# Split inputs computed ahead and kept in DRAM, the seven-product down projection in block one too, and the sample's modulation sums moved to the projections of blocks two and three

## The chip, the cores and the metric

The kernel runs on one core of a Trainium2 chip. TensorE (PE) multiplies, VectorE (DVE), ScalarE (ACT) and GpSimd (POOL) work elementwise, and SyncE (SP) only issues DMAs; POOL issues DMAs too. Every engine takes its instructions strictly in order, so an instruction that waits holds back all that stands behind it on that engine. The metric is the device time of one execution in microseconds (us), the median of several.

## The reference

One layer of a streaming encoder. A prompt of 2048 tokens and a sample of 64 tokens, each with its own conditioning vector `c`, go through the same weights:

```
mod = silu(c) @ w_ada + b_ada                 # sh1, sc1, g1, sh2, sc2, g2, 1024 each
hn  = rms(x) * (1 + sc1) + sh1
q, f, iv, og, xr, gr = split(hn @ w_in)       # 1024 -> 3072
o_hg = hgrn2(q, f, iv) * gain * silu(og)      # 4 heads of 128, chunks of 64, a state per head
o_rg = rglru(conv(xr)) * gelu(gr)             # width-4 conv, gated linear recurrence
x = x + g1 * (concat(o_hg, o_rg) @ w_out)
x = x + g2 * (relu(hn2 @ w_up)**2 @ w_down)   # hn2 = rms(x) * (1 + sc2) + sh2; 1024 -> 4096 -> 1024
y = rms(x) * final_gain
```

All of it is float32 at a tight tolerance.

## The kernel before, in words

**Split products.** A float32 matrix product is made of three passes over two rounded parts, hi and lo, of each operand (hi·hi, hi·lo, lo·hi). `Split` holds such a pair. Weights are split by ACT (hi, line 244) and DVE or POOL (lo, line 245) out of a raw tile; the split parts of `w_in` and `w_out` are stored to DRAM in block 0 (`kept_in`, `kept_out`) and read back by POOL's queue in the later blocks (`load_kept`, 1 MB each, a ring of six weight tiles `wt`).

**Blocks.** The prompt runs in four blocks b = 0 to 3 of 512 tokens; the title counts them from one, all else by b. The sample rides along in the last. A block has these stages: the input XT (normalised, modulated, split); the projections (`hg_proj` for q and f, `hg_vo` for iv and og, `rg_in`, `rg_out`, lines 651 and 768) with the HGRN chain of each head between them (on PE lines 821 to 905, on DVE a level-by-level chain over seven doubling levels, lines 846 to 858); the output projection and second norm (`phase_O`); the MLP in eight groups g of 512 hidden columns, each with an up projection U(g) (`phase_U`, 96 matmuls of 128x512) and, one group later, its down projection D(g). I call what is left of a block's D work after U(7), up to the next block's first projection, its tail.

**Down projection.** In block 0 `phase_D0` does it plainly: 96 matmuls per group, each of eight PSUM results added to `acc` by DVE (line 1069). In blocks 1 to 3 `phase_W` does it with seven products of half-size blocks in place of eight: 84 matmuls per group (line 1098), with sums of the operand made by `sums_of`, differences of the weights by `down_units` (line 1037), and 14 additions into `acc` and `accM` on DVE (line 1087). `combine` (line 1116) adds these at the end. The last block's last group is plain.

**The next block's input.** `phase_A1` takes the square sums of the next block's x during U(5). `phase_A`, which stands in the tail, multiplies the reciprocal norms out with four matmuls (line 530, `ps_rs`), loads x transposed (`x_t`), and writes hi and lo of XT: per 128 columns one DVE scalar_tensor_tensor (line 540), one ACT activation (541) and another DVE scalar_tensor_tensor (542), 8 of each. They can only begin when U(7) has read the old XT.

**Modulation.** Sums over `w_ada` are made on DVE: a raw tile of 512 KB is multiplied by silu(c) and added up (`ada_first` line 288, `ada_part` line 333, 128x1024), and at the end PE sums over partitions with narrow matmuls against a vector of ones (lines 303 and 337). Part G2 of the prompt's and all six of the sample's (`ada_s`) run in block 0's MLP, eleven steps behind each of the groups 1 to 6, with raw tiles from a ring of two (`rowp`).

**Order.** Each stage has a rank (`sec(b, rank)`); a scheduler sorts every engine's stream by it and by what is ready, so its result is read from the order of instructions, not from the source. SP issues the loads of raw weights, of x and of `w_ada` in order; POOL issues the kept weights.

Of the kernel before, what the change touches and what calls it, by code (L numbers as in the profile page):

```python
# [129 lines left out]
def hymba_step(ctx: ExitStack, tc: tile.TileContext, i: dict, o: dict):  # L130
# [376 lines left out]
    def phase_A1(B, after=None):  # L507

        ss = smp.tile([P, 8], F32, tag="ss", name="ss_a")
        for t in range(4):  # L510
            x = x_load(xp[B.toks[t][4]:B.toks[t][4] + P], P, after)
            S.activation(x, x, AF.Square, accum_out=ss[:, t:t + 1])
        V.tensor_scalar(ss[:, 0:4], ss[:, 0:4], 1.0 / D, EPS, op0=ALU.mult, op1=ALU.add)
        B.rs = rsqrt(ss, P, 4)

    def phase_A(B, after=None):


# [8 lines left out]
        hd = hdp.tile([P, 2560], F32, tag="hd", name="hd_a")  # L527
        ps = pax.tile([P, 512], F32, tag="ax", name="ps_rs")
        for t in range(4):
            T.matmul(ps[:, t * P:(t + 1) * P], lhsT=B.rs[:, t:t + 1].to_broadcast([P, P]), rhs=ident, start=True, stop=True)  # L530
        rb = hd[:, 0:BLK]
        xts = [x_load(i["x_t"][B.b, k2], P, after, hd[:, k2 * D - 1536:k2 * D - 512] if k2 > 1 else None) for k2 in range(4)]
        S.copy(rb, ps)
        for k2 in range(4):
            x = xts[k2].rearrange("p (k t) -> p k t", k=2)
            for kk in range(2):
                k = 2 * k2 + kk
                sc, sh = modc[:, SC1, 0, k:k + 1], modc[:, SH1, 0, k:k + 1]
                hi, lo = (y[:, k, :BLK] for y in B.XT.p)
                V.scalar_tensor_tensor(x[:, kk], x[:, kk], sc, rb, op0=ALU.mult, op1=ALU.mult)  # L540
                S.activation(hi, x[:, kk], AF.Identity, bias=sh)
                V.scalar_tensor_tensor(lo, x[:, kk], sh, hi.bitcast(F32), op0=ALU.add, op1=ALU.subtract)
# [797 lines left out]
```

## Time and profile before

| | us |
|---|---|
| median of 3 runs | 2664.72 (2662.12 to 2667.94) |
| the profiled execution | 2663.96 |
| its span, first to last instruction | 2662.1 |
| mean granted TensorE clock | 0.965 of 2.4 GHz |
| TensorE busy | 2468.7 (93%) |
| VectorE busy | 1812.4 (68%) |

The span is what the trace covers; 1.9 us of the execution lie outside it. TensorE's share says that nearly all time is matmuls or waits of matmuls: a stage gets shorter if its matmuls get fewer or if something that TensorE waits for comes sooner. Stages are read from TensorE's timeline, which gives the first matmul of each.

### The profile page before, as it was taken

To read this page: it belongs to the slowest core of one execution; us is meant where nothing else is said; L and a number is where in the kernel's file an instruction comes from. 1 tells how busy PE (TensorE), PEld (TensorE's weight loads), DVE (VectorE), ACT (ScalarE), POOL (GpSimd) and SP (SyncE) were. 2 spreads that over 40 slices of the span, in tenths; PEclk is the share of its full clock that TensorE was granted. 3 is DMA by queue.
4 is the path that set the end of the run, shared out by engine and by line. 5 is a ranking of instruction groups with operands and counts; after the bars stand their busy time and mean duration, and the time that the engine had idled before them with its cause. 6 is when DMAs were issued, how large, how long until landed. Compare 5 with 4: busy or idle time off the path is not lost.

```text
span 2662.1 us, 33130 instructions
## 1 busy us (share of the span) xinstructions
PE 2468.7 (93%) x12792; PEld 2071.5 (78%) x12792; DVE 1812.4 (68%) x3248; ACT 1026.8 (39%) x1640; POOL 191.5 (7%) x245
## 2 busy tenths in 40 slices
PE   5888899999899999999899999999799998999997
PEld 4667688788787778888677778888678877998976
DVE  7587666766544756878954756878954566568787
ACT  4334252322212336455312336455312524644432
POOL 2311100000011100000001100000011110000000
PEclk8999899999999999999999999999899999999998
DMA  8564735766355332234445332234353533222213
GB/s 337 213 218 155 292 119 199 240 208 208 132 184 205 112 135 84 99 111 166 151 173 211 106 135 83 100 111 146 135 201 127 104 127 131 80 87 88 87 65 107
DMA packets 96414, 397.35 MB, mean 149 GB/s; under 512 B 14432, under 2 KB 16384, under 8 KB 79360
## 3 DMA queue, kind: packets, MB, share of 16 engines
q1 hardware_dynamic: 79696, 274.63, 30.1%
q0 software_dynamic: 16560, 120.59, 12.5%
q8 instruction: 101, 1.65, 0.3%
q14 instruction: 57, 0.47, 0.0%
HBM read 343.77 MB, written 51.41 MB: 148 GB/s over the span
## 4 chain that ended last, share of the span: by engine, by line
PE 66%; DVE 15%; issue 9%; DMA 5%; ACT 4%; POOL 1%; SPq 0%; DVEq 0%; POOLq 0%; ACTq 0%
PE ps_u L1012 24%; PE ps_d L1098 14%; PE ps_in L651 7%; PE ps_d L1064 5%; PE ps_vo L768 4%; PE ps_y L938 3%; DVE wt L245 2%; PE ps_lv L842 2%; DMA raw<-in_w_ada_dram 2%; PE ps_in L636 1%; DMA wt<-kept_in 1%; PE ps_rg L712 1%; PE ps_s L1108 1%; DVE ada_acc L333 1%; DVE ada_acc L288 1%
## 5 line engine op out<-in xcount | busy, mean ns | idle before, releaser
L1012 PE MATMUL ps_u<-XT,wt 128*128 128x512 f32 (+2 forms) x4128 | 749.9, 342 | 18.1 <-ACT XT L399 5.4
L1012 PEld LDWEIGHTS ps_u<-XT,wt 128*128 128x128 f32 x4128 | 658.2, 190 | 101.6 <-ACT XT L399 6.8
L245 DVE TENSOR_TENSOR wt<-raw,wt 128x1024 fp32r<-128x1024 f32 x338 | 414.0, 1237 | 251.6 <-ACT wt L244 220.2
L244 ACT CAST wt<-raw 128x1024 fp32r<-128x1024 f32 x357 | 371.6, 1048 | 316.9 <-PE ps_d L1064 87.1
L651 PE MATMUL ps_in<-XT,wt 128*128 128x512 f32 (+1 forms) x1776 | 376.5, 360 | 13.2 <-POOL wt L245 4.0
L651 PEld LDWEIGHTS ps_in<-XT,wt 128*128 128x128 f32 x1776 | 288.5, 190 | 58.8 <-issue 5.5
L1098 PE MATMUL ps_d<-wt,gS 128*128 128x512 f32 x1104 | 261.6, 395 | 27.2 <-DVE accM L1087 22.8
L1098 PEld LDWEIGHTS ps_d<-wt,gS 128*128 128x128 f32 x1104 | 210.7, 191 | 73.3 <-DVE accM L1087 23.6
L938 PE MATMUL ps_y<-wt,mix 128*128 128x512 f32 x800 | 207.1, 415 | 21.8 <-ACT wt L244 8.4
L1015 ACT ACTIVATE hd_u<-ps_u 128x512 f32<-128x512 f32 (+2 forms) x172 | 85.2, 497 | 343.8 <-PE ps_u L1012 340.0
L768 PE MATMUL ps_vo<-wt,XT 128*128 128x512 f32 x800 | 207.1, 409 | 2.5 <-POOL wt L245 1.6
L938 PEld LDWEIGHTS ps_y<-wt,mix 128*128 128x128 f32 x800 | 156.2, 199 | 61.5 <-ACT wt L244 8.7
L1098 PE MATMUL ps_d<-wt,gA 128*128 128x512 f32 x828 | 196.2, 390 | 0.0
L1064 PE MATMUL ps_d<-wt,gt 128*128 128x512 f32 x768 | 181.0, 396 | 8.3 <-DVE acc L1069 8.3
L1098 PEld LDWEIGHTS ps_d<-wt,gA 128*128 128x128 f32 x828 | 154.9, 188 | 32.0 <-DVE acc L1087 0.2
L1064 PEld LDWEIGHTS ps_d<-wt,gt 128*128 128x128 f32 x768 | 146.9, 192 | 39.9 <-DVE acc L1069 8.9
L768 PEld LDWEIGHTS ps_vo<-wt,XT 128*128 128x128 f32 x800 | 150.2, 195 | 32.3 <-POOL wt L245 1.9
L1037 DVE TENSOR_TENSOR raw<-raw 128x1024 f32<-128x1024 f32 x92 | 113.5, 1233 | 2.2
L1087 DVE TENSOR_TENSOR acc<-acc,ps_d 128x512 f32<-128x512 f32 x160 | 106.2, 681 | 1.7 <-PE ps_d L1098 0.6
L842 PEld LDWEIGHTS ps_lv<-hd_h 128*128 128x128 f32 x640 | 85.6, 204 | 27.5 <-issue 17.7
L1087 DVE TENSOR_TENSOR accM<-accM,ps_d 128x512 f32<-128x512 f32 x120 | 79.9, 681 | 36.5 <-PE ps_d L1098 35.8
L842 PE MATMUL ps_lv<-hd_h 128*128 128x64 f32 x640 | 88.9, 285 | 13.8 <-DVE hd_h L847 11.8
(308 smaller groups left out, 2646.6 us busy)
## 6 DMA issues: line engine op xcount, KB each, us to landing
wt<-kept_in POOLq DMA_DIRECT2D x72, 1024.0 KB, 7.4
raw<-in_w_up_dram SPq DMA_DIRECT2D x128, 512.0 KB, 3.3
raw<-in_w_down_dram SPq DMA_DIRECT2D x128, 512.0 KB, 3.3
raw<-in_w_ada_dram SPq DMA_DIRECT2D x80, 512.0 KB, 4.2
wt<-kept_out POOLq DMA_DIRECT2D x24, 1024.0 KB, 5.1
kept_in<-wt POOLq DMA_DIRECT2D x19, 1024.0 KB, 9.0
raw<-in_w_in_dram SPq DMA_DIRECT2D x24, 512.0 KB, 7.2
x_a<-in_x_prompt_dram SPq DMA_DIRECT2D x16, 512.0 KB, 4.8
```

The lines of the kernel that those rows point to most:

```text
L244: S.copy(wt[:, 0], raw)
L245: eng.tensor_tensor(wt[:, 1], raw, wt[:, 0].bitcast(F32), op=ALU.subtract)
L651: T.matmul(ps[:, :pn], lhsT=w[:, a, k], rhs=B.XT.p[x][:, k, p0:p0 + pn], start=(k == 0 and q == 0), stop=(k == KD - 1 and q == 2))
L768: T.matmul(ps[:rows(B.toks[ti])], lhsT=l, rhs=ws[k // 2][:, a, k % 2], start=(q == 0), stop=(q == len(ops) - 1))
L842: T.matmul(ps[:C, c * C // 2:(c + 1) * C // 2].rearrange("p (b h) -> p b h", h=hs), lhsT=KS[:, c * C:c * C + C], rhs=qv[:, c * bc:(c + 1) ...
L938: T.matmul(ps[:rows(B.toks[ti])], lhsT=l, rhs=ws[k - k % 2][:, a, k % 2], start=(q == 0), stop=(q == len(ops) - 1))
L1012: T.matmul(ps[:, :pn], lhsT=w[:, a, k], rhs=B.XT.p[x][:, k, p0:p0 + pn], start=(k == 0 and q == 0), stop=(k == KD - 1 and q == 2))
L1015: S.activation(r, ps[:, :pn], AF.Relu)
L1037: V.tensor_tensor(d, x, y, op=ALU.subtract)
L1064: T.matmul(ps, lhsT=l, rhs=ws[half][c // 2][:, a, c % 2], start=(q == 0), stop=(q == len(ops) - 1))
L1087: return V.tensor_tensor(dst, dst, ps, op=ALU.add)
L1098: T.matmul(ps, lhsT=op[x][y][:, c, t * P:(t + 1) * P], rhs=w[:, a, c], start=(k == 0), stop=(k == len(ops) - 1))
```

## The change

Three things move.

1. `phase_D0` goes; block 0 uses `phase_W` and `combine` like the others.
2. `keep_A` computes the hi and lo parts of the next block's input ahead, one 128-column step at a time (load, DVE, ACT, DVE, store), and stores them to DRAM (`kept_x`, 4 MB a block). For block 1 it runs in block 0's MLP, four steps a group (G2 after it), with tiles of another ring of two (`xap`) and the stores on POOL's queue; for blocks 2 and 3 in the projections of blocks 1 and 2, with tiles of the ring of three raw weights and the stores on SP's queue. `phase_A` is then eight loads of 512 KB on POOL's queue (and the sample's own norm in the last block).
3. The sample's six modulation parts leave block 0's MLP. `ada_sample(1)` and `ada_sample(2)` make half of them each in the projections of blocks 1 and 2: 24 raw tiles of 512 KB through the same ring of three, 48 DVE operations of 128x512, six sums on PE. G2 of the prompt stays in block 0's MLP.

```diff
+    def ada_sample(b):
+        accs = adp.tile([P, 2, 512], F32, tag="ada", name="ada_acc")
+        def fin(h, acc):
+            ps = pmd.tile([P, 512], F32, tag="md", name="ps_ada")
+            if h < 4:
+                for m in range(2):
+                    for j in range(2):
+                        T.matmul(ps[:, 2 * m + j:2 * m + j + 1], lhsT=acc[:, (2 * j + m) * P:(2 * j + m + 1) * P],
+                                 rhs=ones, start=True, stop=True)
...
+        hs = range(6 * b - 6, 6 * b)
+        for h in hs:
+            acc = accs[:, h % 2]
+            for k0 in range(0, KD, 2):
+                raw = rawp.tile([P, 1024], F32, tag="raw", name="raw")
...
+                for k in range(2):
+                    ck = silc[:, 1, k0 + k:k0 + k + 1]
+                    if k0 + k == 0:
+                        V.tensor_scalar(av, rv[:, k], ck, None, op0=ALU.mult)
+                    else:
+                        V.scalar_tensor_tensor(av, rv[:, k], ck, av, op0=ALU.mult, op1=ALU.add)
+                if k0 == 4 and h > hs[0]:
+                    with sec(b, 13):
+                        fin(h - 1, accs[:, 1 - h % 2])
+        with sec(b, 13):
+            fin(hs[-1], acc)
...
-    def phase_A1(B, after=None):
+    def keep_A(B, pool_, tag, rbp, eng, at):
         ss = smp.tile([P, 8], F32, tag="ss", name="ss_a")
...
+        for k in range(KD):
+            t = pool_.tile([P, 2, BLK], F32R, tag=tag, name="x_k")
+            x, hi = t[:, 0].bitcast(F32), t[:, 1]
+            Q.dma_start(x, i["x_t"][B.b, k // 2][:, k % 2 * BLK:k % 2 * BLK + BLK])
+            sc, sh = modc[:, SC1, 0, k:k + 1], modc[:, SH1, 0, k:k + 1]
+            V.scalar_tensor_tensor(x, x, sc, rb, op0=ALU.mult, op1=ALU.mult)
+            S.activation(hi, x, AF.Identity, bias=sh)
+            V.scalar_tensor_tensor(t[:, 0], x, sh, hi.bitcast(F32), op0=ALU.add, op1=ALU.subtract)
+            eng.dma_start(B.kept[k // 2][:, :, k % 2], t.bitcast(F32))
+            yield
...
     def phase_A(B, after=None):
         B.XT = Split(xtp, "xt", KD, "XT1")
+        for k2 in range(4):
+            for q in range(2):
+                G.dma_start(B.XT.p[q][:, 2 * k2:2 * k2 + 2, :BLK], B.kept[k2][:, 1 - q])
...
-        plain = B.b == 0 or B.last and g == DFF // 512 - 1
+        plain = B.last and g == DFF // 512 - 1
...
-    def phase_D0(B, g, gt):
...
-    ada_s = [ada_part(G2, 0), ada_first(1)] + [ada_part(p, 1) for p in range(2, 6)]
+    ada_0 = [keep_A(blocks[1], xap, "xa", (adp, "ada"), G, ExitStack)] if NB > 1 else []
+    ada_0.append(ada_part(G2, 0, own=True))
...
+        if 0 < b < NB - 1:
+            keep_b = [keep_A(blocks[b + 1], rawp, "raw", (adp, "ada"), Q, lambda: sec(b, 13))]
+            run(keep_b, 2)
...
+        if 0 < b < NB - 1:
+            with sec(b, 30):
+                run(keep_b, 99)
+                ada_sample(b)
...
-                        run(ada_s, 11)
+                        run(ada_0, 4)
...
-                if b:
-                    combine(B)
+                combine(B)
```

Where it moves instructions, three places show it. VectorE, in U(7) of block 1, where its tail begins, before (`hd_a` and `x_a` hold x of the next block, XT_9161 is its input; lines 971 to 975 and 966 are the sums of U(7)):

```order
L1037 TENSOR_TENSOR raw<-raw 128x1024 x2
L245 TENSOR_TENSOR wt<-raw,wt 128x1024 x2
L540 SCALAR_TENSOR_TENSOR x_a<-x_a,modc,hd_a 128x512 x3
L542 SCALAR_TENSOR_TENSOR XT_9161<-x_a,modc,XT_9161 128x512
L966 TENSOR_TENSOR gA_9139<-hd_u,gA_9139 128x512
L542 SCALAR_TENSOR_TENSOR XT_9161<-x_a,modc,XT_9161 128x512 x2
L540 SCALAR_TENSOR_TENSOR x_a<-x_a,modc,hd_a 128x512
L966 TENSOR_TENSOR gA_9142<-hd_u,gA_9142 128x512
L540 SCALAR_TENSOR_TENSOR hd_a<-hd_a,modc 128x512
L971 TENSOR_TENSOR hd_u<-hd_u 128x2x256
```

and now, at the same place (lines 1098, 1027, 1032 and 1127 are the old 1037, 966, 971 and 1087):

```order
L1098 TENSOR_TENSOR raw<-raw 128x1024 x2
L245 TENSOR_TENSOR wt<-raw,wt 128x1024
L1127 TENSOR_TENSOR accM<-accM,ps_d 128x512
L245 TENSOR_TENSOR wt<-raw,wt 128x1024
L1127 TENSOR_TENSOR accM<-accM,ps_d 128x512
L1027 TENSOR_TENSOR gA_9308<-hd_u,gA_9308 128x512
L245 TENSOR_TENSOR wt<-raw,wt 128x1024
L1127 TENSOR_TENSOR acc<-acc,ps_d 128x512
L1027 TENSOR_TENSOR gA_9311<-hd_u,gA_9311 128x512
L1127 TENSOR_TENSOR acc<-acc,ps_d 128x512
L1032 TENSOR_TENSOR hd_u<-hd_u 128x2x256
```

The sixteen scalar_tensor_tensor are gone, and the tail's additions (line 1127), the first of which came behind all sixteen, now begin among the sums of U(7).

VectorE, in the projections of block 1, where head 1's chain passes two of its levels, before (lines 846, 847 and 857 are the chain, line 708 the convolution):

```order
L846 TENSOR_TENSOR hd_h<-hd_h 128x32x8
L847 TENSOR_TENSOR hd_h<-hd_h 128x32x8
L857 COPY_PREDICATED hd_h<-masks,ps_lv 128x32x8
L846 TENSOR_TENSOR hd_h<-hd_h 128x16x16
L847 TENSOR_TENSOR hd_h<-hd_h 128x16x16
```

and now (907, 908, 918 and 769 are the old 846, 847, 857 and 708; line 365 is a step of a sum of the sample's modulation):

```order
L907 TENSOR_TENSOR hd_h<-hd_h 128x32x8
L908 TENSOR_TENSOR hd_h<-hd_h 128x32x8
L918 COPY_PREDICATED hd_h<-masks,ps_lv 128x32x8
L769 SCALAR_TENSOR_TENSOR rgtmp<-rgtmp,cols 128x512
L365 SCALAR_TENSOR_TENSOR ada_acc<-raw,silc,ada_acc 128x512
L907 TENSOR_TENSOR hd_h<-hd_h 128x16x16
```

Between two levels of the chain there is now an operation that waits for a raw tile.

TensorE at the same place, before (line 821 opens head 1's chain, 842 is a level of it):

```order
L651 MATMUL ps_in<-XT_4809,wt 128x512 x57
L821 MATMUL ps_dg<-hd_h 128x128 x4
L651 MATMUL ps_in<-XT_4809,wt 128x512 x5
L842 MATMUL ps_lv<-hd_h 128x64 x4
L651 MATMUL ps_in<-XT_4809,wt 128x512 x6
```

and now (lines 712, 882, 903 are the old 651, 821, 842):

```order
L712 MATMUL ps_in<-XT_4758,wt 128x512 x55
L882 MATMUL ps_dg<-hd_h 128x128 x4
L330 MATMUL ps_ada<-ones,ada_acc 128x1 x4
L712 MATMUL ps_in<-XT_4758,wt 128x512 x4
L903 MATMUL ps_lv<-hd_h 128x64 x4
L712 MATMUL ps_in<-XT_4758,wt 128x512 x8
```

The sums of the sample's modulation (line 330) stand between the chain's matmuls, six groups of four in each of the two blocks; a matmul of the order is two of the trace there.

## Rows read from the trace of the kernel before

**Rows 1.** Page, part 1: engine, busy us (share of the span) x instructions
```profile
PE 2468.7 (93%) x12792; PEld 2071.5 (78%) x12792; DVE 1812.4 (68%) x3248; ACT 1026.8 (39%) x1640; POOL 191.5 (7%) x245
```

**Rows 2.** Timeline, TensorE, block 0's MLP: start us, us, what, [idle before <-releaser]
```profile
389.17 21.92 PE L1064 MATMUL ps_d<-wt,gt 128*128 128x512 f32 x96
...
607.54 2.47 PE L337 MATMUL ps_ada<-ones,ada_acc 128*128 128x1 f32 x16 [1.98 <-DVE ada_acc L333]
...
677.61 1.05 PE L530 MATMUL ps_rs<-ident,rsq 128*128 128x128 f32 x8
...
692.39 40.75 PE L1064 MATMUL ps_d<-wt,gt 128*128 128x512 f32 x168 [8.25 <-DVE acc L1069]
732.98 11.04 PE L651 MATMUL ps_in<-XT,wt 128*128 128x512 f32 x48
```

**Rows 3.** Timeline, TensorE, block 1's MLP, its tail, block 2's first projection
```profile
1028.18 5.60 PE L1098 MATMUL ps_d<-wt,gA 128*128 128x512 f32 x24
...
1272.98 1.05 PE L530 MATMUL ps_rs<-ident,rsq 128*128 128x128 f32 x8
...
1291.97 11.13 PE L1098 MATMUL ps_d<-wt,gS 128*128 128x512 f32 x42 [11.11 <-DVE accM L1087]
...
1316.71 7.10 PE L1098 MATMUL ps_d<-wt,gS 128*128 128x512 f32 x30 [1.38 <-DVE acc L1087]
...
1326.37 11.04 PE L651 MATMUL ps_in<-XT,wt 128*128 128x512 f32 x48
```

**Rows 4.** Timeline, TensorE, the tail between blocks 2 and 3
```profile
1872.21 0.71 PE L390 MATMUL ps_T<-ident,x_a 64*128 64x64 f32 x8
...
1893.89 10.84 PE L1098 MATMUL ps_d<-wt,gS 128*128 128x512 f32 x36 [11.68 <-DVE accM L1087]
...
1930.81 4.38 PE L651 MATMUL ps_in<-XT,wt 128*128 128x288 f32 x32
```

**Rows 5.** Timeline, TensorE, first up projections of blocks 1 and 2
```profile
977.75 0.52 PE L1012 MATMUL ps_u<-XT,wt 128*128 128x256 f32 x3
...
1576.91 0.52 PE L1012 MATMUL ps_u<-XT,wt 128*128 128x256 f32 x3
```

**Rows 6.** Windows: stretch, us, busy (x) by engine, PEclk, DMA share, GB/s
```profile
1128.80:1169.60 40.80, 40.80 (x181) 33.79 (x180) 32.75 (x41) 19.69 (x26) 0.00 (x0) 1.00 0.30 102
1273.00:1326.40 53.40, 40.92 (x178) 33.25 (x177) 51.35 (x71) 19.14 (x26) 2.64 (x5) 0.90 0.36 133
733.00:853.00 120.00, 117.86 (x621) 94.69 (x620) 50.63 (x132) 16.52 (x30) 13.35 (x23) 1.00 0.52 191
794.76:860.47 65.71, 63.57 (x325) 49.59 (x325) 29.28 (x71) 13.18 (x22) 9.40 (x19) 1.00 0.52 192
40.00:60.00 20.00, 17.75 (x77) 14.13 (x75) 18.59 (x39) 7.26 (x9) 6.54 (x5) 0.91 1.01 417
```

**Rows 7.** Groups by line, 440-680 us: xcount, busy us, mean ns, idle
```profile
L1012 PE MATMUL ps_u<-XT,wt 128*128 128x512 f32 x480 | 115.9, 401 | 0.0
...
L333 DVE SCALAR_TENSOR_TENSOR ada_acc<-raw,silc,ada_acc 128x1024 f32<-128x1024 f32 x28 | 35.9, 1281 | 9.4 <-DMA raw<-in_w_ada_dram 9.4
...
L337 PE MATMUL ps_ada<-ones,ada_acc 128*128 128x1 f32 x64 | 8.2, 258 | 3.4 <-DVE ada_acc L333 3.4
```

**Rows 8.** Groups by line, VectorE, 1273 to 1326 us (one of four)
```profile
L542 DVE SCALAR_TENSOR_TENSOR XT<-hd_a,modc,XT 128x512 fp32r<-128x512 f32 x4 | 3.0, 743 | 0.0
```

**Rows 9.** DMA issues, 440 to 680 us: xcount, KB each, median us to landing
```profile
raw<-in_w_ada_dram SPq DMA_DIRECT2D x46, 512.0 KB, 4.3
```

**Rows 10.** DMA issues, 733 to 853 us
```profile
wt<-kept_in POOLq DMA_DIRECT2D x17, 1024.0 KB, 7.4
...
x<-in_x_prompt_dram SPq DMA_DIRECT2D x2, 512.0 KB, 11.9
```

**Rows 11.** Timeline, TensorE, projections of block 1, head 1
```profile
804.80 4.14 PE L651 MATMUL ps_in<-XT,wt 128*128 128x512 f32 x17 [0.20 <-DMA wt<-kept_in]
...
842.88 0.73 PE L651 MATMUL ps_in<-XT,wt 128*128 128x512 f32 x2 [1.41 <-DVE vo L780]
```

More of the change, by code (lines that the diff above doesn't have):

```diff
@@ L505, in x_load @@
         return x
-    def phase_A1(B, after=None):
+    def keep_A(B, pool_, tag, rbp, eng, at):
         ss = smp.tile([P, 8], F32, tag="ss", name="ss_a")
[L510 to L514, printed above, removed]
+        with at():
+            for t in range(4):
+                x = pool_.tile([P, D], F32, tag=tag, name="x_a")
+                Q.dma_start(x, xp[B.toks[t][4]:B.toks[t][4] + P])
+                S.activation(x, x, AF.Square, accum_out=ss[:, t:t + 1])
+        yield
+        with at():
+            V.tensor_scalar(ss[:, 0:4], ss[:, 0:4], 1.0 / D, EPS, op0=ALU.mult, op1=ALU.add)
+            rs = rsqrt(ss, P, 4)
+            ps = pmd.tile([P, 512], F32, tag="md", name="ps_rs")
+            for t in range(4):
+                T.matmul(ps[:, t * P:(t + 1) * P], lhsT=rs[:, t:t + 1].to_broadcast([P, P]), rhs=ident, start=True, stop=True)
+            rb = rbp[0].tile([P, D], F32, tag=rbp[1], name="rb")[:, :BLK]
+            S.copy(rb, ps)
+        yield
+        B.kept = [dr.tile([P, 2, 2, BLK], F32, name=f"kept_x{B.b}{k2}") for k2 in range(4)]
+        for k in range(KD):
[7 more added lines that the diff above has]
+            eng.dma_start(B.kept[k // 2][:, :, k % 2], t.bitcast(F32))
+            yield
     def phase_A(B, after=None):
         B.XT = Split(xtp, "xt", KD, "XT1")
+        for k2 in range(4):
+            for q in range(2):
+                G.dma_start(B.XT.p[q][:, 2 * k2:2 * k2 + 2, :BLK], B.kept[k2][:, 1 - q])
         if B.last:
@@ L526, in phase_A @@
             norm_T(x, hd[:, 0:D], B.XT, BLK, n, 1, SC1, SH1)
[L527 to L542, printed above, removed]
     def phase_A0(B):
@@ L1225, in hymba_step @@
     ivl = []
+    ada_0 = [keep_A(blocks[1], xap, "xa", (adp, "ada"), G, ExitStack)] if NB > 1 else []
+    ada_0.append(ada_part(G2, 0, own=True))
     ada_p = [ada_part(p, 0, None if blocks[0].last else ivl) for p in range(2, 5)]
[L1227 removed]
     if blocks[0].last:
[L1229 to L1230 removed]
+        run([ada_first(0)] + ada_0, 99)
         phase_A(blocks[0])
@@ L1294, in hymba_step @@
                 gts.append(phase_U(B, g))
-            if g == 5 and not B.last:
-                with sec(b, 161):
-                    phase_A1(blocks[b + 1], B.ulast)
             if g == NG - 1 and not B.last:
@@ L1302, in hymba_step @@
                 with sec(b, 115 + 10 * g):
-                    (phase_W if b else phase_D0)(B, g - 1, gts[g - 1])
+                    phase_W(B, g - 1, gts[g - 1])
                 with sec(b, 116 + 10 * g):
                     if b == 0 and g < 7:
-                        run(ada_s, 11)
+                        run(ada_0, 4)
         with sec(b, 195):
-            (phase_D if B.last else phase_W if b else phase_D0)(B, NG - 1, gts[NG - 1])
+            (phase_D if B.last else phase_W)(B, NG - 1, gts[NG - 1])
         if not B.last:
             with sec(b, 196):
-                if b:
-                    combine(B)
+                combine(B)
             with sec(b + 1, 4.5):
```

41 lines of the change are left out of this document (22 added, 19 removed).

## The prediction

> **What bounds the kernel now.** I read the page's busy times first: TensorE is busy 93% of the span, VectorE 68% [rows 1]. So I look for matmuls that go away and for waits of TensorE, stage by stage, on its timeline. Block 1's MLP shows what the change gives to block 0: from the first D to the last matmul of U(7) it takes 1272.98 - 1028.18 = 244.8 us [rows 3], and one group of it 40.80 us in which TensorE never pauses, with VectorE busy 32.75 us [rows 6]. The same six groups of block 0 take 677.61 - 389.17 = 288.4 us [rows 2]. The three tails, from the last U(7) matmul to the next block's first projection, take 55.4 us [rows 2], 53.4 us [rows 3] and 58.6 us [rows 4]. In each TensorE stands still 8 to 12 us for an addition on VectorE, and not because that addition is slow: VectorE is busy 51.35 of the 53.4 us of the second tail [rows 6], and it is in order, so the additions queue behind the next block's input. The projections of blocks 1 and 2 have almost no waits; TensorE is busy 117.86 of the first 120 us, and the DMA engines 0.52 of them [rows 6]. These projections are where the change puts its load. My sum goes against the profiled execution (2663.96 us, 1.9 us of it outside the span), which lies 0.8 us under the median; the differences are then taken from the median, 2664.7.
>
> **What it gains.** (a) Block 0's MLP is 43.6 us longer than block 1's. Of this, 6 x 12 = 72 matmuls at 40.80/180 = 0.227 us make 16.3. The other 27.3 are the modulation: narrow matmuls at 8.2/64 = 0.128 us, waits for their sums such as the 1.98 us, and up projections of 401 ns a matmul rather than less [rows 2, 7]. G2's own sums stay (16 narrow matmuls, 2, and about 1 of wait), and so do the eight matmuls of line 530 (1). VectorE gets 16 operations at 743 ns [rows 8] for the kept input and eight at 1281 ns [rows 7] for G2 on top of its 32.75 us a group: 22 us over five groups, so 37 of 40.8. It fits, but its tiles come through a ring of two, and I allow 3 us, from 0 to 16. Gain 43.6 - 3 - 1 - 3 = **36.6**. The kept input's stores cost POOL's queue nothing: nothing else stands in it there but what follows in the next block.
>
> (b) The tails. Each holds 168 matmuls of seven products, 168 x 0.227 = 38.1 us. With the sixteen operations gone VectorE has 51.35 - 11.9 = 39.5 us of work in a stretch of about that length, but no addition queues behind an input any more, so the 11.11 us wait goes. What is late next is the second, short wait (1.38 us [rows 3]), which I keep: 39.4 us. First tail (192 plain matmuls before): 55.4 - 39.4 = **16.0**. Second: 53.4 - 39.4 = **14.0**. Third, where the sample's own norm stays (0.7 us of transposes and some 1.5 us of wait): 58.6 - 41.6 = **17.0**. The eight loads of the new input wait for the last matmul of U(7) at the head of POOL's queue, and the kept weights queue behind them: 4.2 MB at the 417 GB/s that the start of the kernel shows [rows 6] are 10 us, and with the first 4 MB of weights 20, under 38 us of matmuls. Cost 0; without that cover 10 us a block. Gains together 83.6.
>
> **What it costs.** (c) `combine` and its DVE work now end block 0 too, so block 1's projections start as block 2's do. From first projection to first up projection block 1 takes 244.8 us, block 2 250.5 [rows 2, 3, 5]: **5.8**.
>
> (d) TensorE's share of the sample's sums moves beside the projections: per block 48 narrow matmuls at 0.128 = 6.1, the line-530 matmuls 1.05, a transpose 0.3, so 7.4; two blocks **14.8**.
>
> (e) The waits there, the term that I cannot read off a row. VectorE gets 48 operations for the sample and 16 for the kept input, 64 x 0.743 = 47.6 us a block. In the 65.7 us in which most of them stand it was busy 29.28 us [rows 6], so 36.4 were free against some 36 of the 48: filled to the brim. It is in order, and each operation pair waits for a 512 KB tile out of a ring of three. Behind such an operation stands head 1's chain, for the chain waits TensorE (`ps_lv`), and with it every projection matmul behind; behind TensorE's new sums stand the same. Three parts. First the pace of the tiles: with L us to landing and 1.5 us of use, a ring of three gives one tile every (L + 1.5)/3 us, so 24 of them need 8L + 12 us; against 65.7 us the excess is 8L - 53.7. Landing took 4.3 us in block 0's MLP [rows 9]; in the very stretch where they go now, 1 MB weights took 7.4 and two 512 KB loads on SP 11.9 [rows 10]. At 7.4 the excess is 5.5. Secondly one operation of 0.74 us between seven levels of the chain, 5.2, which the matmuls that fill in there may hide. Thirdly the kept weights: 21 MB more (2.1 of x, 2.1 of x_t, 4.2 of stores, 12.6 of `w_ada`) run beside 22.9 MB, and the weights arrive just in time as it is (a wait of 0.20 us on one [rows 11]); one load 3 us late gives 3. So G = 5.5 + 5.2 + 3 = 14 per block. The ends are 0 (4.3 us, all hidden) and 8 x 11.9 - 53.7 + 8.2 = 50. I take 14, since 7.4 us is the median of 17 loads of this stretch and the 11.9 of two. Two blocks **28**. Stores of the kept input stand on SP's queue and wait for VectorE; behind them stand the same tiles' loads, which are in the ring's pace already.
>
> The rows say how full the queues get: 22.9 MB took a share of 0.52 of 120 us [rows 6], so 44 MB would take all of it, while the kernel's start moved 417 GB/s over 20 us, more than the 366 that 44 MB in 120 us ask for. The Trainium skill's page "DMA: Bandwidth & Descriptors", section Bandwidth, speaks against the change here: it says that between HBM and SBUF the HBM side binds, at about 358 GB/s for a core. By that an estimate of 44/0.358 = 123 us would stand for the stretch, 3 us late in each block, and the forecast below would be 6 us later; the 417 GB/s row disagrees, and the sum goes without it.
>
> Sum: -83.6 + 5.8 + 14.8 + 28 = -35.0, so 2664.7 - 35.0 = **2629.7**, say 2630 us (2629 from the profiled execution).
>
> **The rivals.** R1, the cover holds: the tiles land near 4.3 us and the chain's extra operations lie under projection matmuls. Then G is 0 to 6 and the time 2602 to 2614. For it: the waits of this stretch are short now (1.41 us on VectorE behind the chain [rows 11]), and VectorE's 36.4 free us are just what the sums need. Against it: they leave no room for any wait.
>
> R2, the transfers fill the 16 engines (share near 1.00). Landings of 8.4 to 9.6 us then give G = 22 to 31 and 2646 to 2664. For it: the 0.52. Against it: the 417 GB/s row.
>
> R3, slower. The mechanism is the tiles' landing alone, in the projections of blocks 1 and 2: with everything but G the net is -63.0, so it turns at G = 31.5 a block, that is L = (31.5 - 8.2 + 53.7)/8 = 9.6 us. At the 11.9 us of the two SP loads G is 50, the net +37 and the time 2702. For it: these loads are the same size on the same queue in the same stretch. Against it: two loads only, and both beside a burst of weights at the block's start.
>
> R4, block 0's seven products yield little: with the ring of two VectorE paces the groups, the whole 16.3 of the matmuls is lost, 2646. For it: 37 of 40.8 us on VectorE. Against it: block 1's groups run without a pause at 32.75 [rows 6], and 4 us a group are still free.
>
> **How the numbers follow.** Forecast (G 7 to 20, 2616 to 2642): 0.52. R1: 0.18. R2: 0.12. R3: 0.09, of which 0.02 end within 0.2%. R4: 0.07. Something beyond these: 0.02. The range leaves out the end of R2 and R3: 2602 to 2658. A measurement of this kernel tells about 0.2% (5.3 us) from no change. Faster by more 0.87, within it 0.05 (the end of R2 and the start of R3), slower 0.08.
>
> **What would show it.** Block 0's six groups should take 248 to 256 us. The tails should take 39 to 42 us each, with TensorE's waits in them under 3 us. Block 1's projections should take 244.8 + 5.8 + 7.4 + 14 = 272 us and block 2's 250.5 + 7.4 + 14 = 272, with waits of TensorE on `ps_ada`, `hd_h` and `wt<-kept_in`, and w_ada's tiles landing in some 7 us. Two projections of 255 us would be R1, of 285 R2, over 290 R3. The forecast is wrong if the tails stay above 45 us (then a store or load of the kept input has become late), or if block 0's groups stay above 44 us each.

## The result, and the profile after

The changed kernel takes 2678.06 us (median of 8 runs, 2671.66 to 2686.18) against 2663.09 of the kernel before on the same chip (8 runs): ratio 1.0059, 95% interval 1.0045 to 1.0074. It is 15 us slower, where 35 us faster was forecast, and 20 us above the range. The profiled execution has a span of 2683.3 us, 21.2 more than before.

The page's busy times of the changed kernel, to set beside [rows 1]:

```profile
PE 2475.0 (92%) x12696; PEld 2076.7 (77%) x12696; DVE 1917.0 (71%) x3364; ACT 1085.6 (40%) x1726; POOL 223.1 (8%) x277
```

TensorE has 96 matmuls fewer and is busy 6 us longer. VectorE has 105 us more. The stages, each from the first matmul of the one to the first of the next on TensorE's timelines (the kernel before from [rows 2 to 5]), say where the time went:

| stage | before, us | after, us | difference | forecast |
|---|---|---|---|---|
| start to block 0's first D | 389.2 | 395.5 | +6.3 | 0 |
| block 0's MLP, six groups | 288.4 | 256.3 | -32.2 | -36.6 |
| tail 0 to 1 | 55.4 | 43.6 | -11.8 | -16.0 |
| projections of block 1 | 244.8 | 290.5 | +45.8 | +27.2 |
| tail 1 to 2 | 53.4 | 44.6 | -8.8 | -14.0 |
| projections of block 2 | 250.5 | 283.2 | +32.7 | +21.4 |
| tail 2 to 3 | 58.6 | 46.4 | -12.2 | -17.0 |
| all the rest | 1321.8 | 1323.2 | +1.4 | 0 |
| span | 2662.1 | 2683.3 | +21.2 | -35.0 |

The rows of the first block's stages, TensorE's timeline of the changed kernel (start, length, what it does, in brackets the wait ahead and its releaser):

```profile
395.48 5.60 PE L1138 MATMUL ps_d<-wt,gA 128*128 128x512 f32 x24
...
651.75 5.60 PE L1138 MATMUL ps_d<-wt,gA 128*128 128x512 f32 x24
...
685.58 7.19 PE L1138 MATMUL ps_d<-wt,gS 128*128 128x512 f32 x24 [3.60 <-DVE acc L1127]
...
695.33 11.04 PE L712 MATMUL ps_in<-XT,wt 128*128 128x512 f32 x48
...
985.85 0.51 PE L1073 MATMUL ps_u<-XT,wt 128*128 128x256 f32 x3
```

and the window of block 2's projections (stretch, us, busy by engine, granted clock, DMA share, GB/s):

```profile
1325.55:1608.80 283.25, 253.95 (x1275) 203.51 (x1274) 185.42 (x433) 78.81 (x129) 31.03 (x44) 0.93 0.60 215
```

The first rows answer to [rows 2] and [rows 5]: the long waits of the tail are down to one of 3.60 us, and block 1's projections, which begin at 695.33 rather than 732.98, end after they did.

The gains came, at 0.6 to 0.9 of their size. The projections cost 1.6 times what was put down for them (78.5 us in place of 48.6). TensorE's waits in those of block 1 (line and what it waits for; us in total, times, longest):

```profile
PE ps_oT L966 <- DVE hd_h L962: 7.6, 2, 4.2
PE ps_in L712 <- DVE vo L841: 7.1, 1, 7.1
PE ps_dg L882 <- POOL hd_h L878: 5.9, 2, 3.2
...
PE ps_ada L330 <- DVE ada_acc L365: 1.8, 1, 1.8
```

and VectorE's own for DMA, in the same stretch:

```profile
DVE ada_acc L365 <- DMA raw<-in_w_ada_dram: 20.5, 6, 6.1
...
DVE x_k L585 <- DMA x_k<-in_x_t_dram: 5.4, 2, 4.0
```

VectorE stood 20.5 us for tiles of `w_ada` (21.8 with the first operation of each sum, line 363); in the kernel before no tile of `w_ada` is read there. One such place on VectorE's timeline, at head 1's end (line 841 makes the `vo` that TensorE needs):

```profile
830.71 1.54 DVE L365 SCALAR_TENSOR_TENSOR ada_acc<-raw,silc,ada_acc 128x512 f32<-128x512 f32 x2 [6.11 <-DMA raw<-in_w_ada_dram]
834.87 1.54 DVE L365 SCALAR_TENSOR_TENSOR ada_acc<-raw,silc,ada_acc 128x512 f32<-128x512 f32 x2 [2.61 <-DMA raw<-in_w_ada_dram]
836.32 0.68 DVE L841 TENSOR_TENSOR vo<-vo,ps_vo 128x512 f32<-128x512 f32 x1
841.02 0.75 DVE L365 SCALAR_TENSOR_TENSOR ada_acc<-raw,silc,ada_acc 128x512 f32<-128x512 f32 x1 [4.02 <-DMA raw<-in_w_ada_dram]
841.69 0.35 DVE L962 SCALAR_TENSOR_TENSOR hd_h<-ps_o,rsq,vo 128x128 f32<-128x128 f32 x1
```

and on TensorE's:

```profile
823.07 6.92 PE L829 MATMUL ps_vo<-wt,XT 128*128 128x512 f32 x18
837.06 2.50 PE L712 MATMUL ps_in<-XT,wt 128*128 128x512 f32 x5 [7.07 <-DVE vo L841]
842.09 0.79 PE L942 MATMUL ps_o<-Sst,hd_h 128*128 128x128 f32 x2 [2.53 <-DVE hd_h L962]
842.68 0.63 PE L943 MATMUL ps_o<-vo,hd_h 128*128 128x128 f32 x2
```

VectorE waits 6.11 and 2.61 us for tiles. The matmuls whose result the addition of line 841 needs end at 829.99, and ScalarE's copy of it at 830.62; the addition runs at 836.32, behind the tiles, and TensorE has stood 7.07 us for it. In [rows 11] the same wait is 1.41 us. The matmuls around it are slow as well: a pair of `ps_o` matmuls takes 0.63 us, and 0.39 later in the same trace. The windows of the whole stage before,

```profile
732.98:977.75 244.77, 233.88 (x1217) 185.63 (x1216) 131.02 (x330) 65.27 (x106) 28.39 (x43) 0.99 0.45 160
```

and of the stage, of the stop with the matmuls ahead of it, and of the 11 us at its end and behind it, after:

```profile
695.33:985.85 290.52, 255.23 (x1274) 204.07 (x1273) 185.80 (x433) 78.82 (x130) 30.52 (x43) 0.92 0.59 209
818.00:842.00 24.00, 12.68 (x39) 9.28 (x37) 8.91 (x15) 0.60 (x1) 2.65 (x5) 0.65 1.00 363
836.00:847.00 11.00, 7.41 (x32) 6.36 (x33) 5.40 (x10) 1.11 (x2) 0.00 (x0) 0.56 0.92 337
```

The clock that the throttle granted over the stage fell from 0.99 to 0.92, and in the 11 us behind the longest wait it was 0.56, which is mostly the lower level of 1.2 GHz. It was low before that wait too: 0.61 from 823 to 830 us, where TensorE worked without a pause after a wait of 1.80 us for a sum. So TensorE lost time twice: it was idle 35.3 us in place of 10.9, and busy 21.4 us longer, of which 8.6 are added matmuls (7.26 on `ps_ada`, 1.05 on `ps_rs`, 0.27 a transpose).

The DMA engines were full at the stop (share 1.00, 363 GB/s): five loads of kept weights of 1 MB were issued there between 818.9 and 830.3 us. The tiles of `w_ada` that VectorE waited for landed late among them (KB each, median us to landing of those issued from 819.5 to 825.5; the profile has two of the six, 9.1 and 15.9):

```profile
raw<-in_w_ada_dram SPq DMA_DIRECT2D x6, 256.0 KB, 12.5
```

Block 2 has the same stop: VectorE waited 6.90 us for a tile, with a landing of 14.5 us beside it, and TensorE 7.2 us for `vo`.

### The profile page after: what moved, and what is told of

Same layout as the page of the kernel before. It is cut to its first block, busy times and chain, and to the rows that moved or that the text cites. A ratio compares the mean times of both kernels' runs of the same rounds, so it can differ in the third digit from the quotient of the medians.

```text
span 2683.3 us, 33281 instructions
## 1 busy us (share of the span) xinstructions
PE 2475.0 (92%) x12696; PEld 2076.7 (77%) x12696; DVE 1917.0 (71%) x3364; ACT 1085.6 (40%) x1726; POOL 223.1 (8%) x277
## 4 chain that ended last, share of the span: by engine, by line
PE 64%; DVE 13%; issue 10%; DMA 8%; ACT 3%; POOL 1%; SPq 0%; DVEq 0%; POOLq 0%; ACTq 0%
PE ps_u L1073 25%; PE ps_d L1138 19%; PE ps_in L712 6%; PE ps_vo L829 3%; DMA raw<-in_w_ada_dram 3%; PE ps_y L999 3%; PE ps_lv L903 2%; DVE wt L245 2%; DMA wt<-kept_in 2%; PE ps_in L697 1%; PE ps_s L1148 1%; PE ps_rg L773 1%; DVE ada_acc L365 1%; DVE raw L1098 1%; DVE accM L1127 1%
## 5 line engine op out<-in xcount | busy, mean ns | idle before, releaser
L245 DVE TENSOR_TENSOR wt<-raw,wt 128x1024 fp32r<-128x1024 f32 x362 | 441.7, 1236 | 203.4 <-ACT wt L244 172.0
L1138 PE MATMUL ps_d<-wt,gS 128*128 128x512 f32 x1488 | 353.2, 396 | 15.8 <-DVE acc L1127 11.1
L712 PEld LDWEIGHTS ps_in<-XT,wt 128*128 128x128 f32 x1776 | 296.0, 194 | 77.3 <-DVE vo L841 15.1
L1138 PEld LDWEIGHTS ps_d<-wt,gS 128*128 128x128 f32 x1488 | 283.1, 191 | 80.1 <-issue 12.0
L1138 PE MATMUL ps_d<-wt,gA 128*128 128x512 f32 x1116 | 264.1, 389 | 0.4 <-DVE wt L245 0.4
L1138 PEld LDWEIGHTS ps_d<-wt,gA 128*128 128x128 f32 x1116 | 208.8, 188 | 44.2 <-DVE wt L245 0.8
L1098 DVE TENSOR_TENSOR raw<-raw 128x1024 f32<-128x1024 f32 x124 | 152.5, 1230 | 2.4
L1127 DVE TENSOR_TENSOR accM<-accM,ps_d 128x512 f32<-128x512 f32 x162 | 108.0, 682 | 61.4 <-PE ps_d L1138 61.1
L1127 DVE TENSOR_TENSOR acc<-acc,ps_d 128x512 f32<-128x512 f32 x216 | 144.3, 682 | 1.0
L1026 ACT CAST gS<-hd_u 128x512 fp32r<-128x512 f32 x124 | 76.2, 621 | 96.2 <-PE ps_d L1138 65.1
L907 DVE TENSOR_TENSOR hd_h<-hd_h 128x256 f32<-128x256 f32 x112 | 55.5, 495 | 49.6 <-PE ps_lv L903 43.0
```

Of the source, the lines that this page charges most:

```text
L245: eng.tensor_tensor(wt[:, 1], raw, wt[:, 0].bitcast(F32), op=ALU.subtract)
L712: T.matmul(ps[:, :pn], lhsT=w[:, a, k], rhs=B.XT.p[x][:, k, p0:p0 + pn], start=(k == 0 and q == 0), stop=(k == KD - 1 and q == 2))
L1026: S.copy(t[:, 0], raw)
L1098: V.tensor_tensor(d, x, y, op=ALU.subtract)
L1127: return V.tensor_tensor(dst, dst, ps, op=ALU.add)
L1138: T.matmul(ps, lhsT=op[x][y][:, c, t * P:(t + 1) * P], rhs=w[:, a, c], start=(k == 0), stop=(k == len(ops) - 1))
```

## The experiments

The theory after the result, A: VectorE, in order, waits for each tile of the sample's sums, and behind it wait head 1's chain and TensorE. Rivals: B, the 36 us of added VectorE operations a block fill the engine; C, the added transfers starve the kept weights and everything else. Every ratio is to the kernel before, timed beside it.

### Without the sample's sums

```diff
-        accs = adp.tile([P, 2, 512], F32, tag="ada", name="ada_acc")
...
-                raw = rawp.tile([P, 1024], F32, tag="raw", name="raw")
...
+        if b == 1:
+            V.memset(modc[:, :, 1], 0.25)
```

> The changed kernel without the sample's sums in the projections of blocks 1 and 2: no w_ada tiles, no VectorE operations, no sums on TensorE (the sample's modulation is left out; a constant stands in its place). Theory A (VectorE waits for the tiles, in order, and holds head 1's chain and TensorE), theory B (the 36 us of added VectorE work a block fill the engine) and theory C (the added traffic starves the other loads) all say that the sums cost most of the 73 us by which these projections are longer: 2610 to 2625 us, projections of some 257 us each. If the kept inputs of the next block, which stay, are the cost, the time stays above 2650.

Measured: 2617.8 us, ratio to before 0.9825 (0.9788 to 0.9861). The projections of blocks 1 and 2 take 258.3 and 255.4 us. So the sums cost 60 us of the changed kernel, and the kept inputs' work with `combine` 13.5 us in block 1 and 4.8 in block 2. A single stage is read to some 7 us only: the same work took 262.2 us in block 2 in the run with kept inputs alone, below. All three theories allow this; what it excludes is that the kept inputs or the seven products were the loss in the changed kernel. It also gives a floor: hidden for nothing, the sums would leave a kernel 48 us faster than before.

### The operations without their tiles

```diff
-                raw = rawp.tile([P, 1024], F32, tag="raw", name="raw")
+                xv = blocks[b].XT.p[0][:, k0:k0 + 2, :BLK].bitcast(F32)
...
-                        Q.dma_start(raw[:, j * 512:j * 512 + 512],
-                                    w_ada1[2 * h + j][:, k0:k0 + 2].rearrange("p k c -> p (k c)"))
```

> The changed kernel with the sums' VectorE operations and TensorE sums all there, but reading the block's input from SBUF in place of w_ada tiles: the 24 loads a block are left out (so the sample's modulation is not the reference's). Theory A: the waits go, what stays is 12 us a block (7 of sums, 5 in the chain): about 2635 us. Theory B: hardly faster than the changed kernel, 2665 to 2675. Theory C: as A.

Measured: 2638.2 us, ratio 0.9897 (0.9865 to 0.9928). The window of block 1's projections:

```profile
696.83:959.02 262.19, 243.65 (x1275) 194.98 (x1274) 183.66 (x433) 78.84 (x129) 28.16 (x43) 0.97 0.51 182
```

The instructions of TensorE and VectorE are as many as in the changed kernel (1274 or 1275, and 433), VectorE is busy 183.7 us against 185.8, and the stage is 28 us shorter; block 2's is 16 us shorter (267.1 against 283.2). B falls: the work fits. Of the 28 us, 16.7 are idle time of TensorE and 11.6 are the same matmuls done sooner, with the clock at 0.97 rather than 0.92.

### The tiles with short operations

```diff
+                if h < 4:
+                    rv, av = rv[:, :, :, :32], av[:, :, :32]
+                else:
+                    rv, av = rv[:, :, :64], av[:, :64]
```

> The changed kernel with all 24 loads a block and all sums, but the VectorE operations cut from 512 to 64 columns (the rest of the modulation is left out): about 5 us of VectorE work a block in place of 36. Theory A: VectorE still waits for every tile in the same places, 2655 to 2675. Theory B: 2630 to 2640. Theory C: 2660 to 2675.

Measured: 2673.9 us, ratio 1.0033 (1.0018 to 1.0048): 4 us under the changed kernel and still slower than before. The window, and VectorE's and TensorE's waits in it:

```profile
690.79:973.35 282.56, 252.01 (x1274) 201.65 (x1273) 166.41 (x434) 78.83 (x129) 27.47 (x43) 0.93 0.60 215
```

```profile
DVE ada_acc L370 <- DMA raw<-in_w_ada_dram: 25.1, 11, 8.7
...
DVE ada_acc L368 <- DMA raw<-in_w_ada_dram: 6.0, 3, 3.1
```

```profile
PE ps_ada L337 <- DVE ada_acc L370: 9.8, 1, 9.8
...
PE ps_ada L330 <- DVE ada_acc L370: 5.4, 2, 3.6
```

VectorE is busy 20 us less and waits 31 us for tiles; the stage (282.6 us, and 284.9 in block 2) is about as long as with the full operations. Together with the run above this is the case: the time hangs on the wait and not on the work.

### All transfers, no engine waiting

```diff
+                Q.dma_start(scr[(h % 6) * 4 + k0 // 2], raw[:8])
+                xv = blocks[b].XT.p[0][:, k0:k0 + 2, :BLK].bitcast(F32)
```

The first added line frees the tile, the second is what VectorE reads; the tile and its load stay as in the changed kernel, and the operations' operands are taken from that input.

> All 24 tiles of w_ada a block are loaded through the ring of three as in the changed kernel, but VectorE's operations read the block's input in place of them (so the sample's modulation is not the reference's); a tile's place is freed by a store of 32 KB of it to DRAM, so that no engine but SP waits for a tile. Same transfers, same VectorE work, same sums as in the changed kernel. Theory A (VectorE's wait in order): as without tiles, 2636 to 2648 us. Theory C (the traffic itself): 2660 to 2680.

Measured: 2636.5 us, ratio 0.9898 (0.9872 to 0.9923), as without tiles. The transfers of the stretch from 690 to 890 us, and the sums' operations on VectorE (busy, mean, idle ahead):

```profile
DMA packets 16114, 53.14 MB, mean 266 GB/s; under 512 B 1721, under 2 KB 1729, under 8 KB 12934
...
wt<-kept_in POOLq DMA_DIRECT2D x19, 1024.0 KB, 8.4
```

```profile
L371 DVE SCALAR_TENSOR_TENSOR ada_acc<-XT,silc,ada_acc 128x512 f32<-128x512 f32 x42 | 29.8, 746 | 0.1
```

53 MB moved in these 200 us (51.8 in the changed kernel), the DMA engines had a share of 0.97 from 810 to 835 us, the kept weights took 8.4 us to land, and TensorE waited 1.6 us for one of them: C falls. The two stages take 269.6 and 263.2 us against 262.2 and 267.1 without tiles, 3.4 more together, which single traces cannot tell from nothing. In the changed kernel the same loads look like this (KB each, us to landing):

```profile
wt<-kept_in POOLq DMA_DIRECT2D x19, 1024.0 KB, 7.3
raw<-in_w_ada_dram SPq DMA_DIRECT2D x32, 256.0 KB, 4.8
...
raw<-in_w_ada_dram SPq DMA_DIRECT2D x8, 512.0 KB, 7.5
```

So at the median its tiles landed as the prediction assumed (7.4 us) or sooner: half tiles in 4.8, whole ones in 7.5. But the longest waits lie where the landing was far from the median: 12.5 us among the kept weights at head 1's end, above.

### Five tiles in flight

```diff
-                raw = rawp.tile([P, 1024], F32, tag="raw", name="raw")
+                raw = (xap.tile([P, D], F32, tag="xa", name="raw") if k0 // 2 % 2 else
+                       rawp.tile([P, 1024], F32, tag="raw", name="raw"))
```

> The changed kernel, all of it computed, with the tiles of the sample's sums in the projections taken in turn from the ring of three and from the other ring of two, five in flight in place of three. If the ring's turn (landing plus use over the number of tiles) sets the pace, the tiles come every 1.9 us rather than every 3 and most of VectorE's waits go: 2640 to 2655. If SP's queue (stores of the kept input and loads that wait ahead of the tiles) or the transfers set it, the time stays at 2668 to 2680.

Measured: 2712.3 us, ratio 1.0161 (1.0142 to 1.0181), slower than either expectation. SP's longest waits in block 1's projections and TensorE's for the sums:

```profile
SPq L354 <- DVE rsp L426: 36.4, 1, 36.4
SPq L989 <- DVE vo L842: 35.6, 1, 35.6
```

```profile
PE ps_ada L330 <- DVE ada_acc L366: 18.3, 3, 12.4
PE ps_ada L337 <- DVE ada_acc L366: 9.7, 2, 5.0
```

The deeper ring moved SP's order: after the first ten loads of the sums (line 354) there now stand the output projection's loads of x (line 989), which wait for line 774 (20.4 us) and for `vo`, and SP waits there with all the other sums' loads behind it. It then stood 36.4 us more ahead of the next of them; what kept that one is an inferred releaser and was not taken apart. TensorE now waits 28 us at the sums rather than at `vo` (1.4 us there). So this run does not test the ring's depth, and whether more tiles in flight would hide the landings stays open; it shows a third engine, SP, in which one waiting instruction holds the rest.

### Seven products alone

```diff
-    def ada_part(part, which, after=None, own=False):
+    def ada_part(part, which, after=None, own=True):
...
-        plain = B.b == 0 or B.last and g == DFF // 512 - 1
+        plain = B.last and g == DFF // 512 - 1
...
-                if b:
-                    combine(B)
+                combine(B)
```

The edit is made to the kernel before, and the line numbers are its own; the first pair of lines takes the tiles of the modulation sums from another ring.

> The kernel before with part 1 alone: block 0 with seven products and combine; the next block's input made in the tails and all of the sample's sums in block 0's MLP as before, with their tiles from a ring of two that the weights do not use. VectorE then has 32.8 us a group for the products and some 10 for the modulation, more than the 40.8 us of matmuls. If VectorE sets the pace: block 0's six groups about 275 to 285 us in place of 288.6, block 1's projections 5 us longer for combine, the whole 2655 to 2665 us. The rival, that the matmuls' 16 us are gained whatever VectorE does: 2645 to 2650.

Measured: 2682.8 us, ratio 1.0058 (1.0036 to 1.0079). Block 0's six groups take 301.7 us, 13 more than with plain products:

```profile
PE ps_ada L337 <- DVE ada_acc L333: 15.1, 4, 11.5
PE ps_u L1012 <- DVE wt L245: 5.1, 3, 2.3
```

TensorE waits for the modulation's sums (15.1 us) and now for weights too. So with the sample's sums beside them the seven products lose in block 0, and in the changed kernel, without those sums, they gain; that it is VectorE's time which both need fits, and is argued from these waits. The expectation counted VectorE's work and left out the waits. Block 1's projections take 245.8 us here, only 1.0 more than before, though `combine` stands ahead of them.

### Kept inputs alone

```diff
-        plain = B.last and g == DFF // 512 - 1
+        plain = B.b == 0 or B.last and g == DFF // 512 - 1
...
-    ada_0.append(ada_part(G2, 0, own=True))
+    ada_0 += [ada_part(G2, 0), ada_first(1)] + [ada_part(p, 1) for p in range(2, 6)]
...
-                ada_sample(b)
```

> Part 2 alone: all three inputs computed ahead and kept; block 0 with the plain down projection and all of the sample's sums in its MLP, as before. By the stages of the changed kernel and of the one without the sample's sums: tails shorter by 10, 9 and 12 us, projections of blocks 1 and 2 longer by some 8 and 5, block 0's MLP by 3: about 2648 us (2642 to 2656). A rival, that the kept inputs' traffic and stores cost in the projections what the tails give: 2660 to 2668.

Measured: 2663.7 us, ratio 0.9988 (0.9974 to 1.0002): no difference. The tails give 12, 10 and 12 us, and block 0's MLP (+12), block 1's projections (+8) and block 2's (+12) take them back. The rival gave this time; but it put the whole loss into the projections, and a third of it lies in block 0's MLP.

### The sums in the MLP

```diff
-            ps = pmd.tile([P, 512], F32, tag="md", name="ps_ada")
+            ps = pax.tile([P, 512], F32, tag="ax", name="ps_ada")
...
-                raw = rawp.tile([P, 1024], F32, tag="raw", name="raw")
+                raw = xap.tile([P, D], F32, tag="xa", name="raw")
...
+                    if 0 < b < NB - 1 and g < 8:
+                        run(ada_b, 4)
```

TensorE's sums also get another PSUM ring (`ax`) here, and in the next three versions.

> The changed kernel, all of it computed, with the sample's sums moved on from the projections into the MLP of the same blocks, four tiles a group through the ring of two that the kept input of block 1 uses. There VectorE is busy 32.8 of 40.8 us a group and gets 6 more. Theories A to C: the projections fall to some 257 us as without the sums, TensorE's sums stay (6 us a block): 2622 to 2638 us. The rival for the MLP: waits for tiles from the ring of two cost 2 to 4 us a group, 2645 to 2670.

Measured: 2644.6 us, ratio 0.9927 (0.9899 to 0.9956): faster than both kernels, by 33 us than the changed one. 245 us of block 1's MLP:

```profile
1004.00:1249.00 245.00, 245.00 (x1103) 203.64 (x1102) 209.25 (x262) 122.94 (x169) 0.00 (x0) 1.00 0.39 130
```

TensorE does not stand still at all, and the MLP grows by 4.5 us, which is the sums' matmuls. Of the 48 operations 32 stand in block 1's MLP, and VectorE waits for no tile there, at a DMA share of 0.39: the tiles have landed when it comes to them. What a wait would cost there this run does not show. The other 16 stand ahead of the MLP, at the end of the stage counted as projections, and there VectorE waits again:

```profile
DVE ada_acc L365 <- DMA raw<-in_w_ada_dram: 5.5, 3, 3.0
```

(3.9 us in block 2). The projections take 261.0 and 266.4 us, more than without sums (258.3, 255.4), which puts the time above the expected 2638. TensorE's two waits behind those operations (`ps_oT` and `ps_y`) are 5.2 us longer than without sums in block 1 and 4.5 in block 2; the rest of the 11 us in block 2 was not taken apart.

### The kept inputs in the MLP too

In one version ScalarE multiplies and GpSimd adds for the sums, in the other VectorE does both:

```diff
-                        V.scalar_tensor_tensor(av, rv[:, k], ck, av, op0=ALU.mult, op1=ALU.add)
+                        S.mul(rv[:, k], rv[:, k], ck)
+                        G.tensor_tensor(av, av, rv[:, k], op=ALU.add)
...
+            ada_b = [keep_A(blocks[b + 1], xap, "xa", (adp, "ada"), G, ExitStack), ada_sample(b)]
```

> All of the change's work that it put into the projections of blocks 1 and 2, kept inputs and the sample's sums, moved on into the MLP of the same blocks, with the sums' multiplications on ScalarE and the additions on GpSimd, which is idle there. All is computed. Projections of both blocks at 250.5 us as block 2's before, MLPs of blocks 1 and 2 at 245 to 250 us, tails as in the changed kernel: 2605 to 2618 us. The rival: GpSimd's additions (1.26 us each beside VectorE) or the one ring of two slow the MLPs by more than 8 us each, 2625 to 2645.

> The version with the sample's sums in the MLP (on VectorE), and the kept inputs of blocks 2 and 3 in the same MLPs too, with stores on GpSimd's queue, six steps a group. All is computed. VectorE gets 32.8 + 8 us a group, which just fits 40.8. If it fits: projections at 250.5 us each (10 and 16 less than there), MLPs at 250 to 256 us, the whole 2618 to 2632. If VectorE sets the pace or waits for tiles in the MLP: 2 to 4 us a group more, 2640 to 2670, as where ScalarE and GpSimd made the sums.

Measured: 2669.4 us, ratio 1.0004 (0.9990 to 1.0018), and 2655.4 us, ratio 0.9966 (0.9949 to 0.9982). In both the projections return to 250 us, and in both the MLPs of blocks 1 and 2 grow, by 21 to 27 us. With ScalarE and GpSimd, ScalarE waits 25.9 us for tiles in block 1's MLP. Its longest such wait there, VectorE's and TensorE's (line 1138 is the down projection):

```profile
1089.66 1.33 ACT L365 ACTIVATE raw<-raw,silc 128x512 f32<-128x512 f32 x2 [4.01 <-DMA raw<-in_w_ada_dram]
```

```profile
1092.44 1.77 DVE L245 TENSOR_TENSOR wt<-raw,wt 128x1024 fp32r<-128x1024 f32 x1 [5.46 <-ACT wt L244]
```

```profile
1094.86 5.98 PE L1138 MATMUL ps_d<-wt,gS 128*128 128x512 f32 x18 [5.54 <-DVE accM L1127]
```

ScalarE makes the high part of the weights, in order; while it stood for a tile, VectorE waited for that part, and TensorE for the addition that stands behind the split on VectorE. So at this place the wait went to another engine of TensorE's path. It is 5.5 of the 26 us; the rest was not taken apart. VectorE's steps beside GpSimd's are longer too (two of line 1098 took 3.60 us, 1.22 each elsewhere). With VectorE alone TensorE waits for low parts of weights, and VectorE for the kept input's own loads:

```profile
PE ps_u L1072 <- DVE wt L245: 8.3, 5, 2.6
```

```profile
DVE x_k L584 <- DMA x_k<-in_x_t_dram: 10.7, 3, 4.3
```

Of the 23 us by which block 1's MLP grew there, 9.1 are waits of TensorE; the rest is longer busy time, 57 added matmuls and a granted clock of 0.97 in place of 1.00. That VectorE's work no longer fits there is likely, and not shown.

### Part of the tail's weights on GpSimd

```diff
-        w22 = split_raw(r22, V)
+        w22 = split_raw(r22, G if g == 7 else V)
...
-        t2, t3, t4 = (split_raw(r, V) for r in (r22, r12, r21))
+        t2, t3, t4 = (split_raw(r, G if g == 7 and q == 1 else V) for q, r in enumerate((r22, r12, r21)))
```

> The version with the sample's sums in the MLP, and two of the seven low parts of the last group's weights made by GpSimd in place of VectorE, so that VectorE has 2.4 us less in each tail. If VectorE's 42 us of work set the tails' 43.5 to 46 us: each tail 2 to 3 us shorter, 2636 to 2640. If GpSimd's 2.5 us each or its queue come late: 2645 to 2655.

Measured: 2644.2 us, ratio 0.9927 (0.9900 to 0.9955), no different from the version that it was made from; the tails are 45.3 to 48.3 us, 0.5 to 0.9 longer than there. VectorE's operations in the first tail, and GpSimd's:

```profile
674.84 1.23 DVE L1097 TENSOR_TENSOR raw<-raw 128x1024 f32<-128x1024 f32 x1 [1.69 <-POOL wt L245]
...
679.44 2.78 DVE L245 TENSOR_TENSOR wt<-raw,wt 128x1024 fp32r<-128x1024 f32 x1
```

```profile
678.24 2.90 POOL L245 TENSOR_TENSOR wt<-raw,wt 128x1024 fp32r<-128x1024 f32 x1 [2.88 <-DVE raw L1097]
```

VectorE's next step on the same tile waited for GpSimd, and one of its splits beside GpSimd's took 2.78 us rather than 1.22. So whether less VectorE work shortens a tail stays open. In the changed kernel the addition that TensorE waits for stands behind three splits of the last weights:

```profile
1310.54 3.49 DVE L245 TENSOR_TENSOR wt<-raw,wt 128x1024 fp32r<-128x1024 f32 x3
1313.95 3.07 DVE L1127 TENSOR_TENSOR acc<-acc,ps_d 128x512 f32<-128x512 f32 x5
```

## Why the prediction was wrong, point by point

**What bounds the kernel, and where the load goes** was right: the projections of blocks 1 and 2 decided it, and (e) and the rival that ends slower (R3) named the mechanism, tiles that VectorE waits for in order. **Term (e) was mis-sized.** It allowed 14 us a block. What the projections took beyond (c) and (d) is 45.8 - 5.8 - 7.4 = 32.6 us in block 1 and 32.7 - 7.4 = 25.3 in block 2, 58 in place of 28. The wait for tiles alone is 28 and 16 of it, by the run without tiles; the other 14, by subtraction, lie in the kept inputs' work and the sums themselves. The kept weights, its third part, cost less than put down: TensorE waited 0.5 and 3.7 us for them, 6 were allowed.

The step that failed is the first part of (e), "the excess is 8L - 53.7" at one landing L of 7.4 us. It gave 5.5 us of waits a block; VectorE waited 21.8 us for tiles in block 1 and 18.2 in block 2. Three things in it did not hold. It set the time that 24 tiles need against the whole stretch, as if VectorE's free time were one sum; but a wait holds what stands behind it at that moment, and the free time of another moment does not pay it back. It took a median for every tile; 12.7 of the 21.8 us fell at head 1's end, where tiles landed in 12.5 us among kept weights. And it gave a tile 1.5 us of use: the 24 tiles' loads were issued over some 90 us, where 8L + 12 gives 71 at 7.4 and less at the medians measured, so places in the ring were held longer. These are SP's first and last of them in block 1:

```profile
767.62 0.33 SPq L353 DMA_DIRECT2D raw<-in_w_ada_dram  x1
...
848.83 8.69 SPq L359 DMA_DIRECT2D raw<-in_w_ada_dram  x4
```

With it goes R3's turning point of 9.6 us: the change is slower at median landings of 4.8 and 7.5. **Left out altogether** was the clock: with the waits the granted clock of the stage fell to 0.92, and its matmuls took 11.6 us longer than at 0.97 without tiles. Over the stage 16.7 us of added idle time came with 28.3 us of added time, 1.7 for one.

**(a)** 36.6 was 32.2: 3 us were allowed for the ring in the six groups, and TensorE waits 6.2 there, 4.64 of it once for an addition. 6.3 us more stand ahead of the first D, where the sum did not look. Of these, 3.0 lie between block 0's first up projection and that D. This stretch takes 50.3 us before and 50.4 with seven products alone, but 51.6 to 53.9 in every version with the kept input for block 1, where ScalarE makes the square sums of that input there (line 568) and TensorE's longest wait for ScalarE is 2.1 to 2.6 us:

```profile
357.88 4.34 PE L1073 MATMUL ps_u<-XT,wt 128*128 128x256 f32 x23 [2.47 <-ACT hd_u L1076]
```

So it is the kept input's. The other 3.3 cannot be placed: block 0's projections, the same in all versions, take 315 to 322 us in the traces. That part 1 needs the sums out of block 0's MLP was implied and is shown (+13 us alone).

**(b)** The long waits went as said; 39.4, 39.4 and 41.6 us a tail were 43.6, 44.6 and 46.4, the last above the 45 us that the prediction gave as a sign of being wrong. The first is 40.0 us of matmuls and 3.6 of wait, where the sum had 38.1 and 1.4. The granted clock, 0.96 there, fits the longer matmuls. VectorE is busy 41.7 of the 43.6 us, not 39.5, and the wait kept at 1.38 us is 3.60: before, the long stop ahead of it had let VectorE catch up. That reading is argued from the rows only. **(c)** is uncertain: 1.0 us with seven products alone, 6.1 and 4.8 in the two versions that put nothing else into block 1's projections, 5.8 assumed. **(d)** 7.4 was 8.6 and 8.1 us of matmuls. **R2** (transfers fill the engines) is refuted as a cause by itself: with all transfers, and full engines at head 1's end, nearly nothing was lost where no engine but SP waits for them. By the rule of the Trainium skill's page "DMA: Bandwidth & Descriptors", section Bandwidth (358 GB/s), the prediction's estimate was 3 us a block; the times with and without these transfers, 2636.5 and 2638.2 us, each good to some 7, cannot tell that from nothing. **R1** needed the waits to be hidden, and they weren't. **R4** did not happen: block 0's groups take 40.8 to 42.7 us each but for one of 47.3.

## What to carry to other kernels

Work that has slack on its engine is not free if it waits for a DMA there: ask what stands behind each waiting instruction and who waits for that, and put such work where its loads have landed by the time the engine comes to it (here the MLP, 33 us better than the projections). Sum the waits one by one at their places, with the landing of that place; an average pace against a long stretch takes for granted that free time can be saved up. A wait of TensorE can cost more than its length, so read the granted clock of the stretches around it.
